# Spilled rows of y as room for weight tiles, h in key-block order, initial loads in order of need and new latencies in the scheduler, in a four-layer transformer step

## Chip, cores and metric

One Trainium2 chip, all 8 cores, each running the same program on its own part of the batch. The metric is device time in microseconds (us) of the slowest core, lower is better. A program on eight cores has a second, slower state in some executions (one die at a lower granted clock); only fast runs are compared here. TensorE is called PE in the profile, VectorE DVE, ScalarE ACT, GpSimd POOL, the sync engine's queue SPq.

## The reference, cut to what matters

```python
for l in range(DEPTH):                                   # 4
    sh1, sc1, g1, sh2, sc2, g2 = ada_mod(silu(c), ada_w[l], ada_b[l])   # 1024 x 6144 weights per layer
    h = modulate(y, norm1_g[l], sh1, sc1)                # rms norm, then scale and shift
    if l % 2 == 0:   # even: gated short convolution || neighbourhood attention on a grid
        a, q, k, v = even_proj(h, even_w_in[i], even_conv_w[i], na_q_norm[i], na_k_norm[i])
        mix = concat([a, attention(q, k, v, na_rpb[i])]) @ even_w_out[i]
    else:            # odd: pooling || multi-head latent attention
        p, q, ckv, kpe = odd_proj(h, odd_w_in[i], ...)
        mix = concat([p, attention(q, mla_kv(ckv, kpe, ...))]) @ odd_w_out[i]
    y = y + g1 * mix
    y = y + g2 * sq_relu_mlp(modulate(y, norm2_g[l], sh2, sc2), mlp_w1[l], mlp_w2[l])
```

Each core has 1536 tokens in three blocks of 512: block 0 is context, blocks 1 and 2 are one latent grid of 16 rows of 64 columns. D is 1024. An MLP is 1536 matmuls of 128x512, an even layer's projections are 768 of them.

## The kernel before, the parts that matter

Every instruction is a node with estimated duration and dependencies; a list scheduler puts the nodes in an order for each engine, and the engines then run that order strictly in sequence. Three places matter (cut, marked with `...`).

```python
LAT = {"pe": 0.22, "act": 0.12, "dve": 0.10, "pool": 0.12, "sp": 0.1}   # the scheduler's latencies
DMA_RATE = 0.33e6
...
NW = 2                                     # two slots for weight tiles (1 MB bf16 each), used in turn
def wtile(srcs, key=None):
    s = wt_i[0] % NW
    ...
# even layer: k and v of the latent blocks are put in key-block order after the projection
kin  = kt_[:].rearrange("p (g r b c) -> p b g r c", g=2, r=4, b=2)
kout = kT[:, j, blk(tb)].rearrange("p (g b r c) -> p b g r c", g=2, b=2, r=4)
for b in range(2):
    COPY(kout[:, b], kin[:, b], [bkt], [bk[tb][j]], eng="pool")
...
DMA("sp", prs, [bv], [...], "vx%d" % (vt % 4))    # v: 8 small SBUF-to-SBUF copies per token tile
wts = [wtile(<q>), None, wtile(<v>)]
...                                                # q and v tiles
wts[1] = wtile(<k>)                                # k's weights come into q's slot
...                                                # k tiles, then conv: 4 more wtile()
# start: 14 small constants, all of x, then four modulation tiles through the two slots
```

## Time and profile before

| | before |
|---|---|
| time, fast runs | 2673.85, 2696.95 and 2668.82 us (one slow run 2851.74) |
| span of the profiled run | 2670.9 us |
| PE busy / idle in it | 2343.6 / 327.3 us |
| even layer 0, odd 1, even 2, odd 3 without their MLPs | 431, 294, 302, 296 us |
| four MLPs | 334 to 341 us each |

The line of the page for the engines' busy time, share and number of instructions:

```profile
PE 2343.6 (88%) x13818; PEld 1117.1 (42%) x13818; DVE 1125.4 (42%) x1644; ACT 1079.8 (40%) x1586; POOL 375.1 (14%) x407
```

The table of stretches, PE's list of waits and pieces of the chain are shown in the prediction.

**A measure for layers.** The end of a mixing layer and the first MLP matmuls overlap. So I measure a layer from its first projection to the first projection of the next layer (layer 0 from the start, layer 3 to the end): it contains the layer's MLP. The numbers are medians over the eight cores of the profiled run. Before: 767.7, 630.0, 639.7 and 624.7 us.

### The profile page before, as it was taken

To read this page: it belongs to the slowest core of one execution; us is meant where nothing else is said; L and a number is where in the kernel's file an instruction comes from. 1 tells how busy PE (TensorE), PEld (TensorE's weight loads), DVE (VectorE), ACT (ScalarE), POOL (GpSimd) and SP (SyncE) were. 2 spreads that over 40 slices of the span, in tenths; PEclk is the share of its full clock that TensorE was granted. 3 is DMA by queue.
4 is the path that set the end of the run, shared out by engine and by line. 5 is a ranking of instruction groups with operands and counts; after the bars stand their busy time and mean duration, and the time that the engine had idled before them with its cause. 6 is when DMAs were issued, how large, how long until landed. Compare 5 with 4: busy or idle time off the path is not lost.

```text
span 2670.9 us, 37465 instructions; the slowest of 8 cores (2654.4 to 2670.9 us)
## 1 busy us (share of the span) xinstructions
PE 2343.6 (88%) x13818; PEld 1117.1 (42%) x13818; DVE 1125.4 (42%) x1644; ACT 1079.8 (40%) x1586; POOL 375.1 (14%) x407
## 2 busy tenths in 40 slices
PE   1777768999987788999997798999998779899999
PEld 0334333444443454444443343444444345344444
DVE  0434425444456324443454365544445522444443
ACT  2566514111266595121145576411126659522111
POOL 3111114000013102100012212200001210100000
PEclk9998879999999898999999898999999979999999
DMA  9356794346312205556533546555631220233334
GB/s 172 57 88 124 118 145 64 49 75 101 62 30 32 41 2 74 84 80 95 80 52 53 85 91 106 79 81 87 103 62 31 32 41 2 32 48 48 48 48 126
DMA packets 218706, 188.77 MB, mean 71 GB/s; under 512 B 65632, under 2 KB 208864, under 8 KB 218528
## 3 DMA queue, kind: packets, MB, share of 16 engines
q0 software_dynamic: 177136, 148.42, 37.8%
q1 hardware_dynamic: 41392, 37.96, 5.0%
q8 instruction: 114, 1.87, 0.3%
q14 instruction: 64, 0.52, 0.1%
HBM read 319.39 MB, written 11.67 MB: 124 GB/s over the span
## 4 chain that ended last, share of the span: by engine, by line
PE 72%; DMA 6%; ACT 6%; issue 4%; POOL 4%; DVE 4%; SPq 3%; DVEq 0%; POOLq 0%; ACTq 0%
PE psall L598 72%; ACT arena L622 4%; SPq L679 3%; POOL hT L672 2%; DMA WT<-ada_w 2%; DMA WT<-even_w_in 1%; DMA WT<-mlp_w 1%; DVE arena L633 1%; DVE ntmp L644 1%; ACT rstd L622 1%; PE psall L606 1%; POOL rtmp L633 1%; ACT hT L622 0%; DVE arena L644 0%; POOL arena L633 0%
## 5 line engine op out<-in xcount | busy, mean ns | idle before, releaser
L598 PE MATMUL psall<-hT,WT 128*128 128x512 bf16 x4656 | 1065.5, 387 | 58.1 <-POOL hT L672 23.0
L622 ACT ACTIVATE arena<-psall 128x512 f32<-128x512 f32 (+6 forms) x721 | 470.8, 662 | 1114.0 <-PE psall L598 1055.2
L598 PE MATMUL psall<-arena,WT 128*128 128x512 bf16 x3456 | 759.5, 381 | 3.6 <-DMA WT<-mlp_w 2.0
L598 PEld LDWEIGHTS psall<-hT,WT 128*128 128x128 bf16 x4656 | 458.3, 99 | 618.3 <-issue 108.9
L644 DVE SCALAR_TENSOR_TENSOR yT<-psall,mod,yT 128x512 f32<-128x512 f32 x480 | 359.7, 750 | 463.7 <-PE psall L598 463.5
L598 PEld LDWEIGHTS psall<-arena,WT 128*128 128x128 bf16 x3456 | 337.8, 98 | 412.5 <-issue 12.5
L644 DVE SCALAR_TENSOR_TENSOR arena<-psall,arena 128x512 bf16<-128x512 f32 x384 | 265.3, 691 | 385.4 <-ACT arena L622 385.2
L598 PE MATMUL psall<-arena 128*128 128x65 bf16 (+9 forms) x2872 | 324.9, 261 | 53.9 <-ACT arena L622 23.8
L598 PEld LDWEIGHTS psall<-arena 128*128 128x128 bf16 (+1 forms) x2872 | 183.0, 100 | 183.1 <-issue 98.7
L679 POOL DMA_DIRECT2D WT<-mlp_w x64 | 56.2, 878 | 1262.2 <-PE psall L598 1241.8
L622 ACT ACTIVATE arena<-psall,rk 128x1024 bf16<-128x1024 f32 (+1 forms) x224 | 188.8, 952 | 14.6 <-PE psall L598 14.3
L622 ACT ACTIVATE nsq<-yT 128x1024 bf16<-128x1024 f32 x96 | 98.9, 1053 | 171.9 <-PE psall L598 104.0
L644 DVE SCALAR_TENSOR_TENSOR ntmp<-yT,A,rstd 128x512 f32<-128x512 f32 x192 | 137.6, 751 | 65.0 <-POOL hT L672 45.5
L622 ACT ACTIVATE hT<-ntmp,mod 128x512 bf16<-128x512 f32 x132 | 92.0, 721 | 81.7 <-DVE ntmp L644 81.6
L672 POOL TENSOR_SCALAR hT<-ntmp,mod 128x512 bf16<-128x512 f32 x52 | 100.1, 1924 | 131.7 <-DVE ntmp L644 123.9
L598 PE MATMUL psall<-WT,hT 128*128 128x512 bf16 (+1 forms) x576 | 99.8, 329 | 12.2 <-ACT hT L622 7.2
L622 ACT ACTIVATE rstd<-rstd 128x512 f32<-128x512 f32 (+2 forms) x116 | 79.0, 685 | 6.6 <-ACT rstd L622 0.4
L606 PE MATMUL psall<-ident,arena 128*128 128x128 bf16 (+1 forms) x316 | 30.5, 251 | 50.0 <-POOL arena L633 41.0
L598 PEld LDWEIGHTS psall<-WT,hT 128*128 128x128 bf16 x576 | 45.2, 102 | 65.3 <-issue 25.5
L598 PE MATMUL psall<-nsq,ones 128*128 128x512 bf16 x192 | 57.8, 418 | 16.5 <-ACT nsq L622 16.5
L648 DVE RECIPROCAL smallr<-psall 128x4 f32<-128x4 f32 (+1 forms) x32 | 6.2, 194 | 155.2 <-PE psall L598 154.9
L598 PE MATMUL psall<-sTb,WT 128*128 128x2 bf16 x384 | 11.6, 164 | 65.2 <-DVE gqr_sb L638 46.6
(97 smaller groups left out, 952.5 us busy)
## 6 DMA issues: line engine op xcount, KB each, us to landing
WT<-mlp_w POOLq DMA_DIRECT2D x64, 1024.0 KB, 8.7
arena<-ada_w POOLq DMA_DIRECT2D x36, 1024.0 KB, 13.2
arena<-rpbx SPq DMA_DIRECT2D x64, 240.0 KB, 3.5
WT<-ada_w POOLq DMA_DIRECT2D x12, 1024.0 KB, 13.3
yT<-xT SPq DMA_DIRECT2D x3, 2048.0 KB, 25.9
WT<-even_w_in POOLq DMA_DIRECT2D x6, 1024.0 KB, 9.7
WT<-even_w_in POOLq DMA_DIRECT2D x24, 256.0 KB, 6.3
yT_out<-yT SPq DMA_DIRECT2D x6, 1024.0 KB, 4.2
```

The costliest lines, as they stand in the source:

```text
L598: h.matmul(R(out), lhsT=lhsT, rhs=rhs, start=start, stop=stop, skip_group_check=skip))
L606: fns = [lambda h, o=o, a=a: h.transpose(R(o), a, ident[:, :]) for (o, a) in items]
L622: return lambda h: h.activation(out=R(out), in_=R(in_), func=func, **kw)
L633: P.add(eng, [lambda h: h.tensor_tensor(out=R(out), in0=R(in0), in1=R(in1), op=op)], reads, writes, vdur(fsize(out), eng, isb(out, in0, in ...
L644: P.add("dve", [lambda h: h.scalar_tensor_tensor(out=R(out), in0=R(in0), scalar=scalar, in1=R(in1), op0=op0, op1=op1)], reads, writes, vdu ...
L648: P.add("dve", [lambda h: h.reciprocal(out=R(out), in_=R(in_))], reads, writes, 0.155 + fsize(out) * 0.0083, key=key)
L672: fv = lambda h: h.tensor_scalar(out=out, in0=in_, scalar1=v, scalar2=None, op0=op)
L679: fns = [lambda h, o=o, i_=i_: h.dma_start(out=o, in_=i_) for (o, i_) in pairs]
```

## The change

Its intent: give weight tiles more room and keep helper traffic off the path. While a mixing layer runs, y of blocks 1 and 2 is only needed again at its end. So it is written to DRAM (in layer 0 simply forgotten, x is still there), and its 32 KB per partition hold modulation and convolution weights, staging tiles and, in odd layers, the pooling's input. The norm writes h in the order in which the attention reads keys, so k and v need no copies, and q and the convolution read it back through a permuted view. At the start the constants come as one load, and x in thirds, each behind the weights that are needed before it. The scheduler gets new latencies and durations, and POOL no longer does the norm's shift. The diff's core:

```diff
-    LAT = {"pe": 0.22, "act": 0.12, "dve": 0.10, "pool": 0.12, "sp": 0.1}
-    DMA_RATE = 0.33e6
+    LAT = {"pe": {"act": 0.32, "dve": 0.275, "pool": 0.3, ...}, "act": {"pe": 0.145, ...}, ...}
+    DMA_LAT = 1.9
...   (durations of several operations and of DMAs re-estimated; an engine is not chosen if another ends sooner)
@@ norm
-                SHIFT(hT[:, kc, blk(tb)], tm[:], ...)            # on ACT, DVE or POOL
+                o, i_ = hT[:, kc, blk(tb)], tm[:]
+                if which == 1 and l % 2 == 0 and tb > 0:
+                    o = o.rearrange("p (b r c) -> p r b c", b=2, r=8)
+                    i_ = i_.rearrange("p (r b c) -> p r b c", b=2, r=8)
+                SHIFT(o, i_, ...)                                # on ACT or DVE
+        def spill(l, tb):
+            if l > 0:
+                DMA("sp", [(ysc[tb - 1], yT[:, tb])], by[tb], [bysc[tb - 1]], "sp%d" % tb)
+            return Arena(0, tb)
@@ mlp
+            order = [M[0], M[1], WT[0], WT[1]] * 3 + [WT[0], WT[1], M[0], M[1]]   # four slots
@@ even layer
-            wts = [wtile(<q>), None, wtile(<v>)]      # and k's later, in q's slot
+            wq, wv, wk = WT[0].fill(<q>), WT[1].fill(<v>), ZS.fill(<k>)
+            yar = spill(l, 1)
+            YS = [Slot(yar, n=384), Slot(yar, n=384)]
+            tmr = Ring([yar.take((128, 512), F32, 1, "tm") for _ in range(2)])     # staging of k, v
+            cslot = [YS[0], YS[1], WT[0], WT[1]]      # the convolution's four weight tiles
+            cws = [cwt(0), cwt(1)]
-                    (k: 2 POOL copies per tile; v: eviction and 8 small DMAs per tile)
+                    (k and v evicted straight into place)
@@ start and layers
+        DMA("sp", [(yT[:, 0], <x block 0>)], [], by[0], "x0", key=-10)
+        (four modulation tiles in four slots; wq0, wv0, wk0; x block 1 after wv0, block 2 after wk0)
-            mlp(l, l + 1 < depth)                     # all 12 modulation tiles of layer l + 1 inside
+            odd_layer(l, ada[l][1])                   # 8 of the 12 now inside the odd layer itself
```

## The prediction

> **What bounds the kernel now.** I compare with the fast runs: 2673.85 and 2696.95 us, and the profiled one, 2672.53 us, with all cores within 17 us at clocks of 0.951 to 0.956; the run of 2851.74 us is the slow state. I read the page's busy shares first (PE 88%, DVE 42%, ACT 40%), then the 40 slices, where PE drops to 1 to 8 tenths in four places, and then cut the span at those places: the even layer 0 with the start, its MLP, odd layer 1, MLP, even layer 2, MLP, odd layer 3, MLP. In this table of stretches the columns after the window are its length and the busy us of PE, weight loads, DVE, ACT and POOL, then granted clock, DMA share and GB/s:
>
> ```profile
> 0.00:431.00 431.00, 277.70 (x1672) 129.15 (x1672) 154.03 (x235) 198.92 (x278) 96.93 (x103) 0.90 0.69 114
> 431.00:769.00 338.00, 336.75 (x1781) 155.88 (x1782) 150.57 (x217) 79.27 (x124) 26.98 (x27) 0.99 0.42 65
> 769.00:1063.00 294.00, 238.76 (x1988) 128.26 (x1986) 120.48 (x183) 202.06 (x293) 48.39 (x64) 0.91 0.22 35
> 1063.00:1397.00 334.00, 333.69 (x1848) 155.47 (x1847) 145.98 (x212) 75.56 (x118) 33.79 (x34) 0.99 0.51 78
> 1397.00:1699.00 302.00, 251.96 (x1203) 115.68 (x1202) 144.00 (x206) 183.68 (x262) 77.60 (x75) 0.94 0.50 84
> ```
>
> The MLPs (338+334+341+335 = 1348 us, half the span) are PE end to end at full clock. In the timeline 56 matmuls of 128x512 start in 12.09 us, so one costs 0.2159 us; 1536 of them are 331.6 us. Nothing about weights or buffers can shorten that. The four mixing layers (431+294+302+296 = 1323 us) have PE idle 323 us, and what PE does there runs at clocks of 0.90 to 0.94. PE's list of waits for the whole kernel names the causes:
>
> ```profile
> PE psall L598 <- ACT arena L622: 63.2, 112, 4.6
> PE psall L598 <- DVE gqr_sb L638: 46.6, 1, 46.6
> PE psall L606 <- POOL arena L633: 41.0, 11, 7.0
> PE psall L598 <- DVE arena L633: 27.3, 27, 3.7
> PE psall L598 <- POOL hT L672: 24.4, 6, 5.7
> PE psall L598 <- DMA WT<-even_w_in: 20.8, 4, 9.4
> PE psall L598 <- DMA WT<-ada_w: 18.6, 5, 7.6
> PE psall L598 <- DMA arena<-ada_w: 18.0, 2, 11.8
> ...
> PE psall L598 <- DMA WT<-mlp_w: 2.0, 4, 0.7
> ```
>
> The chain that ended last calls 8 us of "DMA WT<-mlp_w" critical in each MLP, but PE waits only 2.0 us there in total: the four-slot rotation in the MLP earns nothing. The chain does show three things that the wait list spreads out: the start, the issuing of V's small copies on the sync queue, and the modulation weights of layer 0:
>
> ```profile
> 10.78 12.58 SPq L679
> ...
> 39.82 5.15 DMA gkr_sb<-gkr
> 49.06 18.20 DMA WT<-ada_w
> ...
> 333.80 26.84 DMA WT<-ada_w
> ```
>
> Between 1433 and 1469 the same chain is 56 pieces "SPq L679" of 0.60 us, one after the other.
>
> **What the skill says.** "DMA: Bandwidth & Descriptors", Rules for kernel authors: coalesce small transfers, under 64 KB one pays mostly overhead. The trace agrees: V's 128 copies of 16 KB take 0.60 us of issue each (about 38 us per even layer) and land 1.9 us later; the small constants of 1 to 96 KB land after 4.8 to 29.9 us because they queue behind x. "TensorE: Matmul & The Clock Gate", Why this matters for your kernels: a PE gap above about 3 us costs the full clock. It agrees: clock 0.55 in 860 to 881, where PE is busy 6.95 of 21 us, 1.00 in the MLP. So each wait removed pays a little twice. "GPSIMD Engine Reference", 3.1, has GPSIMD at about twice DVE's time for two-input elementwise work; here it is the one-input shift that is worse: 1924 ns on POOL, 721 on ACT, 686 on DVE.
>
> **The change, part by part.**
>
> PE's own work first, by counting matmuls at 0.2159 us each (shorter ones by their columns). An even layer has 768 projection matmuls, 24 head norms and 24 norm sums: 176 us; context attention 7, neighbourhood attention 8 x 4.5 = 36: 219 us. An odd layer has about 515 of full size, 111 us; query up-projection 12, transposes and small ones 17, context heads 7, and 80 key chunks that ACT paces at 1.00 us each: about 227 us. The actual even layer 2 is 302 and odd layers are 294 and 296, so their excess is 83 and about 68 each; that is all this change can work on.
>
> 1. *Start of layer 0.* PE's first matmul waits 46.6 us for 14 small loads and x, then the third and fourth modulation tile (two slots) until 67.3; the first projection is at 78. DMA is full for 42 us: from 6.52 MB at 34.8% and 5.54 MB at 60.2% of the first 70 us, a plain MB costs 3.7 us and a casting one 7.6. In order of need: one third of x (2 MB, 7.4) and four modulation tiles (30.4) end at about 40, the norm (8 x 0.75 us on DVE plus latency) at 49, the first projection at about 50. But DMA now gates the next: three weight tiles and the rest of x are 23+15 us more, to about 80. PE can do only the first token block (about 22 us) until then. From 80: 219+10 of modulation, less 29 done by then = 200 us of PE work, plus a remaining excess of 40 as in the other even layer. Layer 0 ends at about 320 in place of 431: **-110**. This contains the 12 us of the last modulation tiles at 333 to 361 (26.8 on the chain), since the 8 tiles get two own slots in spilled y and start early. I keep 5 to 10 us of distrust: 8 modulation tiles (61 us), bias tables (7.7 MB, 28), four conv and two output tiles (45), y again (15) are about 150 us of DMA inside 220.
> 2. *Key-block order.* In each even layer 64 sync DMAs, 8 V evictions and 16 POOL copies (403 ns each) go, because the norm writes h permuted and k and v come out in order. Permuted reads by q and conv are runs of 32 elements; attention already streams runs of 40, 480 columns starting 0.20 us apart, so I expect no PE loss. In layer 2 the q and v phase takes 1404 to 1474, and k to 1530; PE's work in it is 67+7 us of 126. Waits there: ACT 20.7, DVE 4.2, weights 4.6 and 1.6 us, and the lost clock. ACT needs some 55 us in it, so PE bounds it: I expect about 83 us. **-43** for layer 2 (in layer 0 it is part of item 1).
> 3. *Odd layers.* 772 to 880 holds 62 us of PE work in 108; the last 21 us have clock 0.55, waiting for POOL's rotary chain (19.4 us of waits), then 96 matmuls of the pooling projection run alone, 21.9 us. With u in spilled y they fill the earlier gaps, as does context attention, which no longer waits for the statistics of all keys: -27. ACT is busy about 120 of the 168 us to 937, so no more than some 45 could go. Eight modulation tiles come in (32 tiny matmuls, 0.80 us each: 6.4), about +4 in a stage paced by ACT. POOL leaves the tail norm (PE waits 4.1 us at 1063): -4. **-27** each, **-54**.
> 4. *MLP.* Two of them lose those eight tiles: 2 x 6.4 = **-13**. The slots gain at most the 2.0 us.
> 5. *Added:* 4 MB of y stored and 4 MB read back in each odd layer (layer 2: 2 and 2), at 3.7 us per MB some 30 us of DMA in stages with a DMA share of 0.16 to 0.22: hidden. The 52 POOL shifts become ACT or DVE work, about 10 us more per mixing layer on engines that are two thirds busy at most. The scheduler's new latencies reorder everything; I can't work that out and give it zero.
>
> Sum: -110-43-54-13 = -220. From 2671 on the trace: 2451; timed, about 2453.
>
> **Rivals.** *(a) DMA becomes the bound of layer 0.* For it: shares of 1.01 in 334 to 400 and 0.96 at the start; eight cores load at once. It would keep layer 0 near 360: 2493. *(b) The chains on ACT and DVE take the place of the waits removed.* For it: the longest single item is PE waiting for ACT, 63 us, and shifts move onto ACT. If the projections run at ACT's latency, items 2 and 3 give half: about 2500. Against: mean use of ACT in the even layer is 184 of 302. *(c) Slots don't matter and y's reload delays the output projection*, because the sync queue is in order and a reload waits for its last user: 10 us in four layers, 2490. Against: reloads are issued when conv or pooling is over, over 60 us ahead of need. *(d) Better:* gaps close and the clock stays up; with 25 us of excess per layer in place of 40, 2390.
>
> **Range and chances.** Most rivals cost 40 to 50 us and are unlikely together; the upside is 60. So 2375 to 2530. The gain has to shrink to a quarter to be under 2%: faster 0.95, same 0.04, slower 0.01. A median that falls in the slow state would add some per cent.
>
> **What would show it.** First projection at about 50, PE thin until 80, MLP 0 starting near 320; no run of "SPq" in the chain of the even layers; no POOL on h; the 96 pooling matmuls scattered; MLPs within 3 us of 332 + 0.8 per modulation tile; odd layers near 268 and even layer 2 near 260. I am wrong if DMA share is 1 in most of 80 to 250, if permuted 128x512 matmuls start more than 0.22 us apart, or if the odd layers stay above 285.

## The result, and the profile after

The changed kernel is correct and takes 2523.1 us (median of the fast runs 2523.07, 2523.08, 2522.88 and 2554.17; one slow run 2659.38). The run of 2554.17 counts as fast, but two of its cores show clocks of 0.956 and 0.954 where the others have 0.965 to 0.969. The ratio to before is 0.9444, 95% interval 0.9334 to 0.9554; without that run it would be 0.9415. Ratios here are the mean time of one kernel's fast runs over that of the other's of the same rounds, so not quite the ratio of the medians quoted. It is faster, as predicted, by about 150 us in place of 220.

The same views as in the prediction. First the page's line of busy times, of the changed kernel:

```profile
PE 2317.2 (92%) x13818; PEld 1113.9 (44%) x13818; DVE 1184.8 (47%) x1748; ACT 1070.4 (42%) x1607; POOL 256.4 (10%) x344
```

Of a span of 2521.4 us PE idles 204.2, before 327.3. PE's busy time hardly moved: 26 us. The table of stretches, changed kernel, the four mixing layers (window, length, busy us of PE, weight loads, DVE, ACT, POOL, granted clock, DMA share, GB/s):

```profile
0.00:365.00 365.00, 277.28 (x1673) 131.45 (x1674) 183.45 (x275) 201.55 (x289) 59.48 (x67) 0.93 0.84 140
692.00:976.00 284.00, 243.57 (x2259) 135.41 (x2257) 135.45 (x220) 203.14 (x303) 48.02 (x78) 0.94 0.56 98
1308.00:1583.00 275.00, 250.53 (x1276) 118.63 (x1275) 157.51 (x225) 183.50 (x268) 45.82 (x48) 0.95 0.57 97
1911.00:2195.00 284.00, 238.41 (x2170) 130.73 (x2167) 134.22 (x216) 202.28 (x302) 43.68 (x73) 0.95 0.46 83
```

Layer 0 lost 66 us of length, but PE is as busy in it as before (277.28 against 277.70); layer 2 lost 27 us, PE busy 250.53 against 251.96. (These windows contain 64 MLP matmuls, 13.8 us, that start ahead of the last gap; before it was 32.) The waits of PE that were longest in total, changed kernel:

```profile
PE psall L610 <- ACT arena L634: 41.6, 93, 3.7
PE psall L610 <- DMA WT<-ada_w: 25.3, 2, 18.9
PE psall L610 <- ACT hT L634: 25.2, 7, 8.6
PE psall L610 <- DVE arena L645: 19.7, 14, 3.7
PE psall L610 <- DMA arena<-ada_w: 15.2, 6, 6.5
```

The waits for the constants (46.6) and for POOL on h (24.4) are gone, those for ACT on the arena (scratch space) are down from 63 to 42, but those for ACT on h, which took over POOL's shifts, are up from 8.8 to 25.2. Summed over the whole lists, PE waited for ACT 91.7 us before and 84.6 after, for DMA 64.6 and 58.9, for DVE 97.4 and 35.6, for POOL 65.4 and 17.9: what went are the constants and POOL. In the measure by layers introduced above:

| us | layer 0 | layer 1 | layer 2 | layer 3 |
|---|---|---|---|---|
| before | 767.7 | 630.0 | 639.7 | 624.7 |
| predicted change, with its MLP | -116 | -27 | -49 | -27 |
| measured after | 694.1 | 615.8 | 598.9 | 602.2 |
| measured change | -73.6 | -14.2 | -40.8 | -22.5 |

(-116 is -110 and half of the MLPs' -13; -49 is -43 and the other half.) So 42 of the missing 70 us are in layer 0, 13 in layer 1, 8 in layer 2, 4 in layer 3.

### The profile page after: what moved, and what is told of

Same layout as the page of the kernel before. It is cut to its first block, busy times and chain, and to the rows that moved or that the text cites. A ratio compares the mean times of both kernels' runs of the same rounds, so it can differ in the third digit from the quotient of the medians.

```text
span 2521.4 us, 37455 instructions; the slowest of 8 cores (2500.1 to 2521.4 us)
## 1 busy us (share of the span) xinstructions
PE 2317.2 (92%) x13818; PEld 1113.9 (44%) x13818; DVE 1184.8 (47%) x1748; ACT 1070.4 (42%) x1607; POOL 256.4 (10%) x344
## 4 chain that ended last, share of the span: by engine, by line
PE 80%; DMA 8%; ACT 5%; issue 3%; DVE 2%; POOL 2%; ACTq 0%; POOLq 0%; DVEq 0%; SPq 0%
PE psall L610 79%; ACT arena L634 3%; DMA yT<-ada_w 2%; DMA WT<-even_w_out 1%; DMA WT<-even_w_in 1%; DMA arena<-rpbx 1%; DMA WT<-ada_w 1%; DMA arena<-ada_w 1%; ACT rstd L634 1%; DMA arena<-PA 1%; POOL rtmp L645 1%; DVE arena L645 1%; DMA yT<-xT 1%; ACT hT L634 1%; PE psall L618 0%
## 5 line engine op out<-in xcount | busy, mean ns | idle before, releaser
L610 PE MATMUL psall<-arena,WT 128*128 128x512 bf16 x2688 | 593.0, 382 | 16.1 <-DMA WT<-even_w_out 8.6
L610 PE MATMUL psall<-hT,arena 128*128 128x512 bf16 x2520 | 565.2, 385 | 15.6 <-ACT hT L634 15.6
L610 PE MATMUL psall<-arena 128*128 128x65 bf16 (+7 forms) x3272 | 477.4, 296 | 57.3 <-ACT arena L634 33.7
L610 PE MATMUL psall<-hT,WT 128*128 128x512 bf16 x1872 | 431.5, 386 | 11.7 <-ACT hT L634 8.6
L610 PEld LDWEIGHTS psall<-arena,WT 128*128 128x128 bf16 x2688 | 263.9, 98 | 336.7 <-issue 25.9
L610 PEld LDWEIGHTS psall<-hT,arena 128*128 128x128 bf16 x2520 | 248.4, 99 | 319.1 <-issue 33.0
L610 PEld LDWEIGHTS psall<-hT,WT 128*128 128x128 bf16 x1872 | 183.4, 99 | 229.4 <-issue 26.7
L634 ACT ACTIVATE arena<-psall,rk 128x1024 bf16<-128x1024 f32 x160 | 166.1, 1119 | 29.0 <-PE psall L610 28.4
L656 DVE SCALAR_TENSOR_TENSOR ntmp<-yT,A,nrstd 128x512 f32<-128x512 f32 x192 | 135.9, 745 | 21.4 <-ACT nrstd L634 14.9
L634 ACT ACTIVATE hT<-ntmp,mod 128x512 bf16<-128x512 f32 x176 | 121.2, 718 | 46.6 <-DVE ntmp L656 45.9
L610 PE MATMUL psall<-hT,yT 128*128 128x512 bf16 x288 | 68.0, 379 | 0.0
L694 DVE TENSOR_TENSOR nsq<-yT 128x1024 bf16<-128x1024 f32 x41 | 50.0, 1223 | 14.6 <-PE psall L610 11.8
```

Source lines behind the costliest of these rows:

```text
L610: h.matmul(R(out), lhsT=lhsT, rhs=rhs, start=start, stop=stop, skip_group_check=skip))
L634: return lambda h: h.activation(out=R(out), in_=R(in_), func=func, **kw)
L656: P.add("dve", [lambda h: h.scalar_tensor_tensor(out=R(out), in0=R(in0), scalar=scalar, in1=R(in1), op0=op0, op1=op1)], reads, writes, vdu ...
L694: "dve": [lambda h: h.tensor_tensor(out=R(out), in0=R(in_), in1=R(in_), op=ALU.mult)]}, reads, writes,
```

## The experiments

Fourteen runs, all with eight cores; labels are e1 to e14. The time is the median of the fast runs. The change itself was not run again in the rounds of the experiments; e4 and e8, whose layers all came back within 3.3 us of its own (2522.5 and 2525.3 us), show that times of different rounds compare that well.

| run | what | time us | ratio to before | layers 0 / 1 / 2 / 3 us |
|---|---|---|---|---|
| after | the change | 2523.1 | 0.9444 | 694.1 / 615.8 / 598.9 / 602.2 |
| e1_hold | convolution held back until k is done | 2514.2 | 0.9418 | 694.8 / 614.3 / 590.5 / 601.9 |
| e2_vtmp | v's staging out of y, layer 0 | 2517.6 | 0.9423 | 684.8 / 616.9 / 601.5 / 601.5 |
| e3_kb_alone | before + key-block order | 2650.4 | 0.9922 | 749.4 / 633.6 / 627.7 / 623.9 |
| e4_spill2x | spill and reload doubled | 2522.5 | 0.9454 | 692.8 / 614.1 / 602.2 / 600.7 |
| e5_old_sched | after, order by the old latencies | 2552.2 | 0.9544 | 708.2 / 616.0 / 612.8 / 600.3 |
| e6_kb_sched | before + key-block order + new latencies | 2641.6 | 0.9866 | 753.1 / 634.1 / 619.6 / 625.0 |
| e7_mod_in_mlp | modulation tiles back in the MLPs | 2518.3 | 0.9406 | 703.7 / 606.1 / 608.2 / 592.4 |
| e8_x_at_once | x requested at once | 2525.3 | 0.9434 | 693.8 / 616.0 / 601.2 / 604.6 |
| e9_less_dma | 6 MB less into layer 0 (wrong result) | 2501.7 | 0.9321 | 676.3 / 616.7 / 598.4 / 601.7 |
| e10_conv_2slots | convolution's two extra slots taken away | 2506.8 | 0.9336 | 695.3 / 609.2 / 592.2 / 595.2 |
| e11_mlp_2slots | MLP with two slots | 2542.1 | none given | 695.1 / 620.3 / 604.7 / 610.1 |
| e12_vtmp_conv2 | e2 and e10 together | 2491.7 | 0.9289 | 679.0 / 615.2 / 591.0 / 595.1 |
| e13_conv2_less_dma | e12 and e9 together (wrong result) | 2486.0 | 0.9247 | 676.6 / 614.7 / 591.6 / 594.3 |
| e14_late_mod | e12, two tiles of layer 0 in its MLP | 2494.1 | 0.9300 | 678.2 / 614.3 / 593.0 / 595.6 |

For e3 the profiled run was slow on one die; its layers are the medians of the four cores of the other die, whose clocks were 0.950 to 0.958.

### e1: hold the filler back

(Filler: independent matmuls with which PE bridges the waits of another phase.)

```diff
-                MMK(out, [... for kc in range(8)], [bw] + bh[tb], [pt.b])
+                MMK(out, [... for kc in range(8)], [bw] + bh[tb] + hold, [pt.b])   # conv: hold = [last k tile]
```

> The changed kernel with one edit: every projection of the convolution also depends on the last k tile, so it cannot be used to fill the q, k and v phase. My theory (filler spent too early): in layer 2 the attention phase (1432 to 1524, PE busy 74.7 of 92 us) has no filler left because two of the four convolution groups (about 15.5 us of matmuls each) ran in the q, k and v phase. With them held back, PE should be full over the heads, and the stretch from the end of MLP 1 to the start of MLP 2 should fall by 8 to 15 us, layer 0 by a similar amount (234 to 306 has PE busy 50.9 of 72): about 2500 us, between 2490 and 2513. Rival (the work only moves): the q, k and v phase alone is paced by ScalarE and VectorE (88 and 68 us busy in 124) and idles by what the heads gain: no change, 2517 to 2530.

Layer 2 fell by 8.4 us as expected, layer 0 not at all; with 2514.2 us the kernel is just outside the range. The table of stretches from the first projection of layer 2 to its MLP, on the slowest core, changed kernel:

```profile
1316.80:1582.60 265.80, 241.33 (x1234) 114.45 (x1233) 153.12 (x220) 177.53 (x258) 37.87 (x45) 0.95 0.58 98
```

and with the convolution held back:

```profile
1314.80:1568.80 254.00, 233.58 (x1234) 111.55 (x1233) 153.12 (x220) 177.39 (x257) 37.61 (x45) 0.99 0.60 102
```

These are the same 1234 matmuls. Of 11.8 us on these two cores only 4.0 are idle time (24.5 against 20.4); 7.8 are PE's busy time, at a granted clock of 0.99 in place of 0.95. (Medians over the eight cores, for layer 2 with its MLP: busy 568.4 and 562.2, idle 29.9 and 26.9.) The heads' phase tells where (windows of the q, k, v phase and of the heads), changed kernel:

```profile
1308.00:1432.00 124.00, 122.99 (x602) 58.64 (x600) 68.29 (x100) 87.77 (x141) 30.42 (x28) 1.00 0.47 82
1432.00:1524.00 92.00, 74.68 (x369) 35.76 (x370) 54.99 (x77) 70.34 (x91) 8.71 (x10) 0.91 0.46 93
```

and the heads with the convolution held back:

```profile
1430.00:1520.00 90.00, 86.81 (x443) 41.84 (x441) 57.30 (x81) 55.95 (x72) 10.85 (x15) 1.00 0.62 117
```

In the changed kernel the convolution's weights arrive early, its matmuls fill the q, k and v phase without a gap, and the heads, which keep ACT busy for 70 of their 92 us and DVE for 55 with exponentials, bias products and divisions, then have too little beside them. A gain in one phase was given back in the next. In layer 0 the rival held: PE is busy 66.7 of 72 us in the heads (234 to 306) in place of 50.9, but 71.7 of 91 in 83 to 174, where it was busy throughout.

### e2: where v's staging tiles lie

```diff
-            tmr = Ring([yar.take((128, 512), F32, 1, "tm") for _ in range(2)])
+            tmr = (the same) if l > 0 else Ring([(cgb[:, 0:512], bcg[0]), (cgb[:, 512:1024], bcg[1])])
```

> The changed kernel with one edit: in layer 0 the two staging tiles through which v and k of the first token block go to DRAM lie in the convolution's buffers instead of in the spilled rows of y of block 1. My theory: these tiles tied the first v tiles to the norm of block 1, which waits for x to land at 67 us; the v weights are there at 53. So the 4 v tiles (32 matmuls, 6.9 us) should start before 65 instead of at 72.4 and layer 0 should end 4 to 8 us earlier: about 2517 us (2513 to 2520). Rival (loads bound the end of layer 0 anyway, DMA share 1.03 in 83 to 130, 0.93 in 174 to 234, 0.97 in 306 to 365): v starts earlier, layer 0 ends where it did, 2521 to 2525.

v's first tile started at 55.8 us (median of the cores) in place of 72.4, and layer 0 is 9.3 us shorter, a little more than expected (the kernel: 2517.6 us). The chain of waits of the changed kernel shows what it was tied to:

```profile
27.78 25.44 DMA WT<-even_w_in
53.30 13.71 DMA yT<-xT
```

v's weights land at 53.2, then PE waits for x of block 1. The timeline of PE there (start, duration, instructions), changed kernel:

```profile
62.25 0.38 PE L610 MATMUL psall<-arena,bdiag 128*128 128x512 bf16 x1 [0.84 <-ACT arena L634]
68.29 1.86 PE L610 MATMUL psall<-nsq,ones 128*128 128x512 bf16 x4 [5.67 <-ACT nsq L634]
70.60 2.05 PE L610 MATMUL psall<-nsq,ones 128*128 128x512 bf16 x4 [0.44 <-ACT nsq L634]
72.44 4.41 PE L610 MATMUL psall<-WT,hT 128*128 128x512 bf16 x16
```

The last line is v (WT stands ahead of hT among its inputs). It comes after the norm sums of block 1 (the lines before it), although it needs nothing of block 1: the two staging tiles for v's copy to DRAM were put into y of block 1, so they were free only when that block's x had come and its norm had read it. The scheduler holds a matmul back until everything that empties its accumulator can be had, so the whole tile waited. A spilled region is only free when its last reader is done; here that put the latest load of the start in front of work that had its inputs.

### e3: the key-block order alone

On the kernel before:

```diff
-                SHIFT(hT[:, kc, blk(tb)], tm[:], ...)
+                SHIFT(o, i_, ...)                       # o, i_ permuted in even layers, as in the change
-                    (k: 2 POOL copies per tile; v: eviction and 8 small DMAs per tile)
+                    (k and v evicted straight into place; q and conv read h through the permuted view)
```

> The kernel before with the key-block order alone (h written permuted, k and v come out in order; the 128 small copies and the 32 POOL copies are gone; loads, slots, spill and scheduler as before). If this part is what I said, layer 2 shortens by 43 us, layer 0 by a good part of that, since the loads bind it less after the start: 2600 to 2630 us. If the two-engine latencies take the place of the copies (layer 2 in the full change lost only 29 us), layer 2 loses 25 to 30 us and layer 0 10 to 20: 2625 to 2650. If the order were worth nothing by itself: 2660 to 2690.

2650.4 us: layer 2 only 12.0 us shorter and layer 0 18.3, at the weak end. All copies are gone from it, so the copies' removal as such gave 12, not 43.

### e4: the spill doubled

```diff
+                DMA("sp", [(ysd[tb - 1], yT[:, tb])], by[tb], [bysd[tb - 1]], "sq%d" % tb)
...
+                    DMA("sp", [(yT[:, tb, <half>], ysd[tb - 1][:, <half>])], [bysd[tb - 1]], ...)
```

> The changed kernel with every spill and every reload of y done twice (to and from a second scratch tensor): 12 MB more written and 12 MB more read per core. My prediction called the spill hidden. Then doubling it costs under 5 us: 2519 to 2528. Rival (spill and reload are on the path at the start or the end of the mixing layers): each of the three layers that spill gets 5 to 15 us longer, 2540 to 2565, and the output projection or the tail of the layer waits for the reload of y.

(The traffic added was 10.5 MB each way, not the 12 I wrote.) 2522.5 us, every layer within 3.3 us: spill and reload are hidden, as predicted.

### e5: the old latencies in the scheduler

```diff
-    LAT = {"pe": {"act": 0.32, "dve": 0.275, ...}, ...}
+    LAT = {"pe": 0.22, "act": 0.12, "dve": 0.10, "pool": 0.12, "sp": 0.1}
...    (and the durations and the choice of engine, as before; SHIFT still without POOL)
```

> The changed kernel, but its instructions put in order with the latencies and durations of the kernel before (the moves of buffers, loads, key-block order and the ban of POOL on the shifts stay). My prediction gave the new latencies zero: then 2517 to 2530 us. Rival (the order is a real part of the gain: the key-block order alone shortened layer 2 by 12 us, the whole change by 34 net of its modulation tiles): each mixing layer gets 5 to 15 us longer, 2545 to 2580 us, layer 2 most.

2552.2 us: 29 us longer, 14.1 in layer 0, 13.9 in layer 2, 2 or less in the odd layers. My zero for the scheduler was wrong; the order of instructions, with the choice of engine that goes with it, is worth 29 us, in the even layers alone.

### e6: key-block order and new latencies

```diff
@@ on e3
-    LAT = {"pe": 0.22, "act": 0.12, "dve": 0.10, "pool": 0.12, "sp": 0.1}
+    LAT = {"pe": {"act": 0.32, "dve": 0.275, ...}, ...}      # with the new durations, SHIFT without POOL
```

> The kernel before with the key-block order and also the changed kernel's latencies, durations and ban of POOL on the shifts; loads, weight slots and spill as before. The key-block order alone gave 2650 us in its fast runs. If the order of instructions is worth zero: 2642 to 2655. If it is what makes layer 2 of the changed kernel another 22 us shorter: 2590 to 2625, with layer 2 from its first projection to the next layer's at about 606 us instead of 628. If instead the slots (weights of k and of the convolution early) make those 22 us, layer 2 stays at 622 to 630.

2641.6 us, layer 2 at 619.6: 8 us from the order of instructions (with POOL's shifts moved), no more. The wait list of PE and the chain for layer 2 of this kernel say what stands in the place of the copies (waits: total, number, longest; chain: start, us, what):

```profile
PE psall L601 <- DMA WT<-even_w_in: 18.9, 2, 9.8
```

```profile
1438.76 11.07 DMA WT<-even_w_in
...
1497.53 14.38 DMA WT<-even_w_in
```

These are the weights of k and of the first convolution tile, which can only be requested when a slot of the two is free. Before, these waits for such weights in this stage were 4.6 us; they lay beside the copies. In the changed kernel they are gone, k's weights having a third slot: that is most likely the rest of layer 2's gain, but no run takes this slot alone away.

### e7: modulation tiles back in the MLPs

```diff
-                odd_layer(l, ada[l][1])
+                odd_layer(l)
-            mlp(l, l + 1 == depth, ada[l + 1][0] + (ada[l + 1][1] if l % 2 else []))
+            mlp(l, l + 1 == depth, ada[l + 1][0] + ada[l + 1][1])
```

> The changed kernel with the eight second-half modulation tiles of layers 1 and 3 put back into the MLPs before them (32 matmuls of 0.80 us in four tiles make 0.8 us each). I predicted that moving them into the odd layers takes 6.4 us from each of two MLPs and costs 4 in each odd layer. Then moving them back costs 2 us each: 2525 to 2530. What the traces show so far (latent attention 8 us longer with them in) would make it a wash or a small gain: 2518 to 2524. In both cases the MLP before gets 6 to 7 us longer.

2518.3 us. Both odd layers are 9.7 and 9.8 us shorter, the layers before them 9.6 and 9.3 longer: a wash. Eight tiles cost 10 us in an odd layer, where I had said 4, and leaving an MLP saves 9.5, where I had said 6.4. Without them the odd layers would stand 23.9 and 32.3 us below those of before, around the 31 that my items for them add up to.

### e8: all of x at once

```diff
-            DMA("sp", [(yT[:, tb], <x block tb>)], [dep], by[tb], "x%d" % tb, key=-9 + tb)
+            DMA("sp", [(yT[:, tb], <x block tb>)], [], by[tb], "x%d" % tb, key=-10)
```

> The changed kernel with all three thirds of x requested at the start again, instead of the second and third only after the first weights. The order of need: by 3.7 us per plain MB the 4 MB moved ahead put the first projection back by about 15 us, from 50 to 65. If the loads as a whole bound the start until 83 us, layer 0 ends the same or up to 5 us later (the norms of blocks 1 and 2 come earlier, the weights later): 2520 to 2528. If the early first projection is worth what it moves: layer 0 ends 10 to 15 us later, 2533 to 2538.

The first projection moved from 49.7 to 64.3 us (medians), as expected, and layer 0 ended where it did: 693.8 against 694.1. The early first projection, whose time I had predicted right, is worth nothing by itself.

### e9: less DMA in layer 0

```diff
-                    w, bw = slots(nt).fill([(0, 512, src)])
+                    w, bw = slots(nt).fill([(0, 128, src[:, :, 0:128])] if lite else [(0, 512, src)])
```

(and the matmuls read that quarter four times; wrong result)

> The changed kernel with a wrong result on purpose: in layer 0 each of the eight second-half modulation tiles loads a quarter of its columns and uses that quarter four times. That takes 6 of 8 MB of converting transfers out of layer 0, 46 us of DMA time by the 7.6 us that such a MB took in the trace of before; the matmuls stay the same in number and shape. My theory of layer 0 (PE's own busy time of 236 us after 83 us, at clocks of 0.86 to 1.00, and 32 us of idle time, most of it in the heads): DMA is not the bound, layer 0 with its MLP gets 0 to 8 us shorter (the wait of 4.3 us for a modulation tile near the end goes): 2515 to 2523. Rival (DMA bounds layer 0 after 83 us, my rival (a)): 20 to 40 us shorter, 2483 to 2503.

Layer 0 is 17.8 us shorter, between the two. The table of stretches for the heads of layer 0, changed kernel:

```profile
234.00:266.00 32.00, 26.52 (x137) 12.83 (x135) 15.79 (x25) 16.49 (x21) 0.87 (x1) 0.89 0.59 146
266.00:306.00 40.00, 24.34 (x112) 10.75 (x111) 23.49 (x36) 33.95 (x46) 7.22 (x8) 0.87 0.44 89
```

and with less DMA:

```profile
234.00:266.00 32.00, 31.59 (x193) 15.87 (x192) 20.59 (x31) 27.32 (x36) 0.87 (x1) 1.00 0.68 181
266.00:306.00 40.00, 32.88 (x146) 14.28 (x145) 23.12 (x32) 20.64 (x27) 10.07 (x14) 0.87 0.85 111
```

The DMA engines are not full in these windows in either kernel. The gain lies where the heads run short of filler, as in e1. (In 234 to 306 PE is busy 50.9 us in the changed kernel, 64.5 here.) Whether it was the transfers or again the order of work, e13 had to tell.

### e10: the convolution's extra slots taken away

```diff
-            cslot = [YS[0], YS[1], WT[0], WT[1]]
+            cslot = [WT[0], WT[1], WT[0], WT[1]]      # filled after the q, k and v tiles
```

> The changed kernel with the two extra weight slots of the convolution taken away: its four weight tiles go through the two old slots, after the weights of q and v. Theory (filler spent too early, by the early weights): the convolution can no longer fill the q, k and v phase and is there for the heads; layer 2 gets 6 to 12 us shorter as with the held-back convolution (8.4 there), layer 0 -5 to +5: 2508 to 2520. Rival (the slots earn something): PE waits for the convolution's weights, both even layers get 5 to 15 us longer, 2533 to 2553.

2506.8 us, 16 us faster than the change. Layer 2 falls by 6.7 us, as with the held-back filler. Layer 0 does not fall: as in e1, PE is busier in its heads (66.5 of 72 us) and idler in 83 to 174 (busy 71.3 of 91). So two of the slots that the change gained are worth nothing, and in layer 2 probably less than nothing. Layers 1 and 3 fall by 7 each, which neither theory expected. They hold no edit; in the traces PE's matmuls there come in another order than in the changed kernel, and more I can't say. Layer 2's 6.7 us are of the same size; that they are the edit's effect rests on e1.

### e11: the MLP with two slots

```diff
-            order = [M[0], M[1], WT[0], WT[1]] * 3 + [WT[0], WT[1], M[0], M[1]]
+            order = [WT[0], WT[1]] * 8
```

> The changed kernel with the MLP's weights going through two slots in turn in place of four. I predicted that the MLP's slots gain at most 2.0 us in all, since PE waited that long for MLP weights in the kernel before. Then taking them away costs 0 to 5 us: 2522 to 2528, and the layers stay within 2 us each. Rival (with fewer slots each MLP waits at its start and end): 3 to 8 us per layer, 2535 to 2555.

Its fast runs took 2540.94 and 2543.30 us, 19 longer (three of five runs were slow, so no ratio is given). Layers 1, 2 and 3 are longer by 4.5, 5.8 and 7.9. My 2.0 us was the wait for MLP weights inside the MLPs, and that is right: here PE waits 0.4 us for them in MLP 1. What the slots pay, they pay elsewhere. With four, the MLP's last tiles leave two slots free and the next layer's first weights come early. The waits at the start of layer 1 of this run (690 to 830 us):

```profile
PE psall L610 <- ACT yT L634: 6.5, 4, 3.1
PE psall L610 <- DMA yT<-odd_w_in: 3.5, 1, 3.5
```

In the changed kernel there is no wait for the layer's own weights in that stretch. Over the starts of layers 1, 2 and 3 such waits in this run's list come to 12.6 us (4.5, 3.3 and 4.8); the other 6 us are not traced to anything.

### e12: e2 and e10 together

```diff
+            tmr = (the same) if l > 0 else Ring([(cgb[:, 0:512], bcg[0]), (cgb[:, 512:1024], bcg[1])])
+            cslot = [WT[0], WT[1], WT[0], WT[1]]
```

> Two edits together, a candidate that should beat both kernels: v's staging tiles out of the spilled y in layer 0 (9 us shorter by itself) and the convolution's weights through two slots. If the two add: layer 0 with its MLP at 680 to 690 us, layer 2 at 588 to 593, in all 2500 to 2510. If the two-slot convolution is no gain: 2514 to 2530.

2489.84, 2498.44 and 2491.72 us, ratio to before 0.9289 (0.9223 to 0.9355): a right result, 31 us faster than the change and better than the 2500 to 2510 expected. Layer 0 is at 679.0, layer 2 at 591.0; layer 3 is again 7 us shorter without an edit, which I count as luck.

### e13: both causes in layer 0 at once

```diff
@@ on e12
+                    w, bw = slots(nt).fill([(0, 128, src[:, :, 0:128])] if lite else [(0, 512, src)])
```

> The two edits of the last candidate (v's staging tiles, convolution through two slots) together with the lightened modulation transfers of layer 0 (wrong result on purpose). Layer 0 with its MLP took 694 us in the changed kernel, 685 with v's staging moved, 676 with 46 us of DMA time taken out, 679 in the candidate; I predicted 652. If the staging and the transfers are two separate causes, they add: 658 to 664 us, and the kernel 2470 to 2480. If they are the same loss seen twice (layer 0 waits for its transfers late in either case): 672 to 679, 2487 to 2498.

Layer 0 took 676.6 us, e12 without the lightened transfers 679.0. They do not add: with v early and the convolution late, 46 us less DMA takes no more than 2 us from layer 0, where e9 gained 17.8. The heads of layer 0 show why; e12:

```profile
234.00:306.00 72.00, 67.51 (x387) 33.35 (x393) 47.26 (x69) 47.42 (x60) 10.82 (x15) 0.98 0.80 136
```

and with less DMA:

```profile
234.00:306.00 72.00, 68.11 (x341) 32.76 (x339) 49.52 (x69) 49.58 (x63) 11.67 (x16) 0.98 0.70 108
```

In e12 the heads are nearly full already, so there was little left for e9's edit to fill. What e9 gained was the same loss, the heads running without filler, seen from the side of the transfers. In both runs PE now idles in 83 to 174 instead (busy 73.6 and 75.0 of 91 us), the longest waits being for two transfers, a modulation tile and a weight tile: 12.8 us in e12 and still 11.8 in e13, where the DMA share of that stretch is only 0.67. The DMA engines were not full there; whether these transfers were asked for too late or queued behind one another no run separates. The kernel's 2487.09 and 2484.82 us are within 14 us of all of e12's fast runs (medians 2486.0 and 2491.7).

### e14: two modulation tiles later

```diff
+        late = ada[0][1][6:8]
-        even_layer(0, ada[0][1], ...)
+        even_layer(0, ada[0][1][:6] + ada[0][1][8:], ...)
-            mlp(l, l + 1 == depth, ada[l + 1][0] + ...)
+            mlp(l, l + 1 == depth, (late if l == 0 else []) + ada[l + 1][0] + ...)
```

> The last candidate, and the last two modulation tiles of layer 0 (the gate of its MLP, needed only at the end of that MLP's first quarter) are loaded and multiplied in MLP 0 instead of in layer 0, with a right result. That takes a quarter of the transfers out of layer 0 that the lightened run showed to be worth 18 us there for three quarters of 8 MB, and gives MLP 0 two tiles of 0.8 to 1.2 us: layer 0 with its MLP 3 to 5 us shorter than the candidate's 679 us, the kernel 2484 to 2495 us. Rival (transfers at the end of layer 0 are not what was waited for): no change, 2490 to 2500 us.

2494.1 us against e12's 2491.7, layer 0 678.2 against 679.0: no change, the rival holds.

## Why the prediction was right and where it failed

The direction and most mechanisms were right: first projection at 49.7 us (50 said), PE thin until 82.6 (80 said), no run of SPq and no POOL on h, permuted 128x512 matmuls 0.216 us apart, the spill hidden. The size was 149.5 us on the trace in place of 220. Other signs failed: MLP 0 starts at 365 us (320 said), even layer 2 takes 275 (260), the odd layers 284 (268, and 285 was to prove me wrong). By its own steps:

**Layer 0, -110: the step that failed is "200 us of PE work".** From 83 us to the start of MLP 0 (365 us, less 13.8 us of MLP matmuls already done) the changed kernel takes 268 us: PE busy 235.8 and idle 32.4. The line that this rests on:

```profile
83.00:365.00 282.00, 249.63 (x1473) 120.38 (x1472) 153.64 (x229) 171.71 (x248) 34.76 (x44) 0.94 0.80 130
```

I had said 200 and 40. The start is right, the idle time is a little better than said, the work is 36 too small. The matmuls of this stretch, counted by their columns at the prediction's rate, come to some 217 us (an estimate from the trace's own list of matmuls). That splits the 36 in two. Some 18 us are PE busy beyond the count: I had counted matmuls at full clock, and the granted clock here is 0.94, which alone makes some 15 (estimate: 6% of 249.6 busy us). The other 17 are work that I had counted as done or not at all: of the 29 us of matmuls that I took as done by 80, only some 19 were (PE was busy 27.7 us by 83, at a clock of 0.81 from 50 on; v's first tiles came only at 72.4, e2), and I had left out the 24 sums of the second norm (5 us) and 3 us of modulation. A further 7 us was in the baseline: the 431 contain 32 MLP matmuls that the 320 do not. The warning stood in my own first table: PE was busy 277.70 us in layer 0 before, and no part of the change takes PE work away from it.

How much of this could be won? e12 took 15 us back by keeping filler for the heads and freeing v, and in e13 taking 46 us of transfers out gave next to nothing more, so rival (a), at 360 us and close to the outcome, would have been right by number and wrong by reason as far as these transfers tell. The other 27 us of layer 0 no run recovered.

**Key-block order, -43 in layer 2: too large by about 11, and right in part for reasons that I had not named.** By itself it gave 12 (e3), since the next wait in line, weights of k and convolution through two slots, took the place of the copies (e6: 18.9 us). With the order of instructions (8, e6) and, most likely, k's third slot, layer 2 got to -40.8, of which 9.3 are the eight modulation tiles that left its MLP (e7), so about -31.5. The step that failed is that 126 us of q, k and v hold only 74 of PE work and can shrink to 83. PE was busy 96.0 of these 126 us:

```profile
1404.00:1530.00 126.00, 96.04 (x420) 41.59 (x420) 46.39 (x63) 69.57 (x111) 36.29 (x40) 0.92 0.43 66
```

It idled 30, less than the 43 that I wanted; some 20 of the 96 are matmuls of the convolution and of the context heads that ran here as filler and would have had to run elsewhere. In the same way I took the layer's 302 us less 219 of ideal work as 83 us of excess to work on. Of these PE idled 50. The rest is the lower clock and matmuls of the neighbouring MLPs inside my window. e1 shows that the clock's part is real and can be had, there by filling gaps: same matmuls, 7.8 us less busy time.

**Odd layers, -27 each: -14.2 and -22.5.** The eight modulation tiles cost 10 us each layer, not 4 (e7). In a layer paced by ACT I had counted their matmuls as partly hidden; they were not. The rest, -31 each said, is -23.9 and -32.3.

**MLP, -13:** -18.9 for the tiles (e7), given back in the odd layers to the last us. The slots, "at most 2.0 us", were read in the right list and the wrong place: taking two away costs 19 us, of which 12.6 are waits at the start of the next layer (e11).

**The scheduler's latencies, zero:** 29 us, in the even layers (e5). So the parts that I did price fell short by more than the total shows: it was luck that an item put at zero made up for some of it.

Some readings of the prediction were off without mattering: its four windows have PE idle 317 us, not 323, the run of SPq is 48 pieces up to 1465.6, not 56, and ACT is busy 110 us in 769 to 937, not 120.

So rival (b) was nearest in kind: ACT and DVE in the heads took the place of the waits removed, and PE's waits for ACT as a whole only fell from 91.7 to 84.6 us. That ACT and DVE are the bound there was not tested by a run that makes them faster. "Perfetto Trace Analysis", Identifying the Most-Contended Engine, warns that matmul busy share does not tell how near PE is to its limit. The same 1234 matmuls had 241.33 and 233.58 busy us.

What stays open: the 7 us that layers 1 and 3 lose in e10, the 6 us of e11 that no wait accounts for, k's third slot by itself, and 27 us of layer 0.

## What to carry to other kernels

Read a stage's gain from PE's idle time in that stage, not from its length less an ideal count: clock loss and borrowed work sit in the difference, and removing a wait does not remove them. Early weights and more slots are not good in themselves: in a kernel with a full phase ahead of a thin one, independent matmuls are worth most in the thin one, so try holding them back (8 us in layer 2, nothing in layer 0, where the first phase then ran dry), and look for what a slot does for the next layer rather than for its own. And before giving a buffer a second life, ask who must have read it first: two staging tiles in spilled rows tied ready work to the last load of the start.

## What the Trainium skill lacked or had wrong

- "GPSIMD Engine Reference", 4.1 Engine selection, calls one-input elementwise work on GPSIMD roughly line-rate. In the kernel before that about holds for a plain cast of 128x512 from f32 to bf16, 762 ns on POOL, but not for the shift of the same shape, which adds one value per partition: 1924 ns on POOL, 721 on ACT and 686 on DVE.
- "TensorE: Matmul & The Clock Gate", Why this matters for your kernels, gives a limit of some 3 us for a gap. The clock of 0.55 where PE was busy 6.95 of 21 us agrees, and so does layer 2: with waits of up to 5.0 us its mean granted clock was 0.95, in e1 with waits of up to 2.8 us 0.99. What I did not find there is a way to price a list of waits; here the difference was 7.8 us of busy time in 241.
- No page that I found gives the rate of a converting transfer beside a plain one. Here a MB took 7.6 us against 3.7 with eight cores loading at once (worked out in the prediction). These are MB as written, in bf16; the source is f32, so two MB are read for each, and per MB read the two are alike: 3.8 and 3.7 us (estimate from the same numbers).
